# Column means of an 8192 x 8192 matrix: the first load divided by partitions

## The chip, the cores and the metric

The kernel runs on one core of a Trainium2 chip. The metric is the device time of one execution in microseconds (us). Before the change three runs took 627.25, 627.92 and 628.02 us; the median is 627.92 us. One more execution was profiled.

Engines are named as in the profile: PE is TensorE, DVE VectorE, ACT ScalarE, POOL GpSimd, SP SyncE. Sixteen DMA engines move the data between HBM and SBUF, the core's memory of 128 partitions.

## The reference

```python
def setup_inputs():
    return {"x": np.random.randn(8192, 8192).astype(np.float32)}

def reference(x):
    return np.mean(x, axis=0)
```

The input is 268.4 MB, the output 32 KB. Every element is read once and added once.

## The kernel before

The 8192 rows are 64 slabs of 128 rows. The first 62 slabs are taken as 31 pairs. For pair k, `rows(k)` (line 59) lays 256 rows out as 128 partitions with two neighbouring rows each, so a partition's share is 16,384 numbers, 64 KB that lie together in HBM. Three buffers of that size, `pairs[0]` to `pairs[2]`, take the pairs in turn.

All loads are issued by the sync queue (SP). `load(k)` (line 77) issues a pair's load: pair 0 in two parts, all partitions' first 2048 numbers (8 KB a partition) and then the remaining 14,336 (56 KB); the last three pairs (`BY_ROW`) in two halves, one row of each partition at a time; every other pair in one transfer of 128 x 64 KB. The loads of pairs 0, 1 and 2 are issued at once (line 87). From pair 3 on the queue first waits until the buffer has been read: `nc.sync.wait_ge(read, k - 2)` (line 95).

VectorE adds. `take(sem, n)` (line 56) waits until a landing semaphore has reached n and subtracts it; every DMA adds 16 when it has landed. The first addition (line 98) folds pair 0's two rows into one, in place. Then for each pair `first_rows` adds the running sum of the buffer before to the pair's first rows, and `second_rows` adds its second rows. `read` is raised behind them and lets the sync queue load the next pair. Each addition is 128 x 8192 numbers at line 54.

The last two slabs come one at a time into the buffer that is free then: the first in four transfers (line 164), the last in ten (line 167). TensorE multiplies the running sum and both slabs by a block of ones and so adds over the partitions into PSUM, piece by piece as the last slab lands; ScalarE and VectorE scale by 1/8192 and three small transfers write the result.

The edit touches only `FIRST` (line 17), `load` and the count in the first `take` (line 97):

```python
FIRST = 2048
...
        cut = FIRST if k == 0 else C if k >= n_pairs - BY_ROW else 2 * C
        for lo, hi in ((0, cut), (cut, 2 * C)):
            if lo < hi:
                sem = second[b] if lo == C else landed[b]
                ins = nc.sync.dma_start(out=pairs[b][:, lo:hi], in_=rows(k)[:, lo:hi])
...
        take(landed[0], 32)
```

## Time and profile before

| | |
|---|---|
| median of three runs | 627.92 us |
| profiled execution, its own time | 627.88 us |
| its span in the profile | 626.1 us |
| DVE busy | 533.5 us, 85% of the span, 67 instructions |
| PE busy | 14.1 us |
| bytes from HBM | 268.44 MB, 429 GB/s over the span |
| one pair addition on DVE, 128 x 8192 | 8.69 us |
| first addition starts | 22.72 us |

Windows and timelines count microseconds from the span's start. A row of a timeline gives start, length, engine, line, operation, output and input, the number of instructions, and in brackets how long the engine was idle before and what ended that. In a list of waits the numbers are the total in us, how many, and the longest. In a list of windows the columns are the stretch, its length, the busy time of PE, PEld (weight loads), DVE, ACT and POOL with the number of instructions, the granted TensorE clock, the busy share of the DMA engines and the GB/s. The bytes of a packet are counted where it starts, so a short window can show more than the engines' mean rate. In a list of DMA issues the numbers are how many, the size of one, and us from issue to landing.

### The profile page before, as it was taken

The numbers are of one execution on the slowest core, as the hardware profiler recorded it, in microseconds if no ns is written. First come the engines' busy times: TensorE is split into PE (matmuls) and PEld (weight loads), VectorE is DVE, ScalarE is ACT, GpSimd is POOL, SyncE is SP. The second block draws the span as 40 slices with busy tenths as digits, with TensorE's granted clock in tenths as the row PEclk, the third lists the DMA queues.
The fourth block names the chain that finished last, engine by engine and source line by source line (L and its number), as shares of the span: only waits on it lengthen the run. The fifth ranks groups of instructions, "written<-read, shape, count | busy, mean of one in ns | idle before, by whom it ended". The sixth has DMA issues, their size and how long they took to land. (4 is left out here: it accounts for less than half of the span.)

```text
span 626.1 us, 524 instructions
## 1 busy us (share of the span) xinstructions
PE 14.1 (2%) x108; PEld 4.8 (1%) x108; DVE 533.5 (85%) x67; ACT 4.2 (1%) x7; POOL 1.0 (0%) x6
## 2 busy tenths in 40 slices
PE   0000000000000000000000000000000000000008
PEld 0000000000000000000000000000000000000002
DVE  0538988889888899888898888988889888899995
ACT  0000000000000000000000000000000000000001
POOL 0000000000000000000000000000000000000000
PEclk9999999999999999999999999999999999999999
DMA  9999999999999999999999999999999999999997
GB/s 404 400 469 402 469 402 465 406 415 456 402 469 402 469 402 469 402 469 402 469 402 469 402 469 402 469 402 456 415 444 427 444 427 415 423 435 435 435 424 316
DMA packets 7115, 268.49 MB, mean 429 GB/s; under 512 B 957, under 2 KB 1473, under 8 KB 1866
## 3 DMA queue, kind: packets, MB, share of 16 engines
q1 hardware_dynamic: 7066, 268.45, 99.3%
q0 software_dynamic: 48, 0.02, 0.0%
q8 instruction: 1, 0.02, 0.0%
HBM read 268.44 MB, written 0.03 MB: 429 GB/s over the span
## 5 line engine op out<-in xcount | busy, mean ns | idle before, releaser
L54 DVE TENSOR_TENSOR pair<-pair,pair 128x8192 f32<-128x8192 f32 (+1 forms) x31 | 263.1, 8486 | 61.5 <-DVEq L57 60.9
L54 DVE TENSOR_TENSOR pair<-pair 128x8192 f32<-128x8192 f32 (+1 forms) x34 | 269.7, 7938 | 23.8 <-DVEq L57 22.7
L136 PE MATMUL wide<-pair,ones 128*32 128x512 f32 (+1 forms) x88 | 12.7, 673 | 609.4 <-DVE pair L54 609.1
L136 PEld LDWEIGHTS wide<-pair,ones 128*32 128x32 f32 x88 | 3.6, 127 | 616.9 <-issue 614.9
L151 ACT ACT_TABLE_LOAD x1 | 1.3, 1283 | 603.4 <-ACTq L112 603.4
L153 DVE TENSOR_SCALAR row<-narrow 1x256 f32<-1x256 f32 x2 | 0.8, 415 | 4.8 <-PE narrow L136 4.8
L136 PE MATMUL narrow<-pair,ones 128*32 128x256 f32 (+3 forms) x20 | 3.5, 387 | 0.0
L151 ACT ACTIVATE rw<-wide 128x512 f32<-128x512 f32 x3 | 1.8, 597 | 15.5 <-PE wide L136 15.5
L199 POOL DMA_DIRECT2D out_dram<-rw x1 | 0.7, 695 | 621.4 <-ACT rw L151 621.4
L136 PEld LDWEIGHTS narrow<-pair,ones 128*32 128x32 f32 x20 | 1.4, 108 | 1.6 <-issue 0.6
L151 ACT ACTIVATE row<-narrow 1x256 f32<-1x256 f32 x2 | 0.8, 377 | 0.5 <-PE narrow L136 0.5
L151 ACT ACTIVATE r<-wide 128x256 f32<-128x256 f32 x1 | 0.4, 384 | 0.3 <-PE wide L136 0.3
L92 POOL MEMSET ones<- 128x32 f32 x1 | 0.1, 124 | 0.3 <-POOLq L230 0.3
L230 POOL MEMSET const-float32-0.0<- 128x1 f32 x1 | 0.1, 98 | 0.2 <-issue 0.2
L230 POOL MEMSET const-float32-1.0<- 128x1 f32 x1 | 0.1, 98 | 0.0
L230 POOL MEMSET const-bfloat16-1.0<- 128x1 bf16 x1 | 0.1, 98 | 0.0
L230 POOL MEMSET const-uint8-127<- 128x1 uint8 x1 | 0.1, 98 | 0.0
## 6 DMA issues: line engine op xcount, KB each, us to landing
pair<-in_x_dram SPq DMA_DIRECT2D x6, 4096.0 KB, 25.6
pair<-in_x_dram SPq DMA_DIRECT2D x7, 1024.0 KB, 11.6
pair<-in_x_dram SPq DMA_DIRECT2D x1, 7168.0 KB, 21.4
pair<-in_x_dram SPq DMA_DIRECT2D x3, 512.0 KB, 16.0
pair<-in_x_dram SPq DMA_DIRECT2D x27, 29.7
pair<-in_x_dram SPq DMA_DIRECT2D x3, 128.0 KB, 11.8
pair<-in_x_dram SPq DMA_DIRECT2D x1, 80.0 KB, 7.4
pair<-in_x_dram SPq DMA_DIRECT2D x1, 48.0 KB, 5.3
```

The lines of the kernel that those rows point to most:

```text
L54: return nc.vector.tensor_tensor(out=dst, in0=a, in1=b, op=ADD)
L92: tc.declare_fence(nc.gpsimd.memset(ones, 1.0).ins, group="ahead")
L136: nc.tensor.matmul(out=dst, lhsT=ones, rhs=src, skip_group_check=True, **flags)
L151: nc.scalar.mul(out=dst, in_=src, mul=inv_r)
L153: nc.vector.tensor_scalar(out=dst, in0=src, scalar1=inv_r, scalar2=None, op0=mybir.AluOpType.mult)
L199: nc.gpsimd.dma_start(out=out[0:W3].rearrange("(n g w) -> g n w", g=GROUPS, w=512), in_=rw.rearrange("(g r) (n w) -> g r n w", r=32, w=512 ...
L230: nc = _bacc.Bacc("TRN2", target_bir_lowering=False, num_devices=1)
```

## The change

Pair 0's load is divided in another way. Before, it was cut by columns, and both parts covered all 128 partitions. After, there are three transfers: partitions 0 to 15 with their first 4096 numbers (16 KB each, 256 KB together), partitions 16 to 127 with their whole 64 KB (7 MB), and the remaining 48 KB of each of partitions 0 to 15 (768 KB). All three raise `landed[0]` by 16, so the first addition waits for 48 in place of 32. The loads of all other pairs and all that follows stay as they were; the order of instructions on PE, DVE, ACT and POOL is the same, and SP issues one transfer more.

```diff
-FIRST = 2048
+FIRST = (16, 4096)
...
     def load(k):
         b = k % 3
-        cut = FIRST if k == 0 else C if k >= n_pairs - BY_ROW else 2 * C
-        for lo, hi in ((0, cut), (cut, 2 * C)):
-            if lo < hi:
-                sem = second[b] if lo == C else landed[b]
-                ins = nc.sync.dma_start(out=pairs[b][:, lo:hi], in_=rows(k)[:, lo:hi])
-                yield ins.then_inc(sem, 16)
+        parts = [(0, P, 0, 2 * C)]
+        if k == 0:
+            p, w = FIRST
+            parts = [(0, p, 0, w), (p, P, 0, 2 * C), (0, p, w, 2 * C)]
+        elif k >= n_pairs - BY_ROW:
+            parts = [(0, P, 0, C), (0, P, C, 2 * C)]
+        for p, q, lo, hi in parts:
+            ins = nc.sync.dma_start(out=pairs[b][p:q, lo:hi], in_=rows(k)[p:q, lo:hi])
+            yield ins.then_inc(second[b] if lo == C else landed[b], 16)
...
-        take(landed[0], 32)
+        take(landed[0], 48)
```

## The prediction

> **What bounds the kernel now.** I read three things: the page's DMA rows, to see whether the transfer engines ever rest; the waits of VectorE and of the load queue, to see who waits for whom; and the first microseconds, because only the first pair's load is edited.

> The page, parts 2 and 3:

> ```profile
> DVE  0538988889888899888898888988889888899995
> DMA  9999999999999999999999999999999999999997
> q1 hardware_dynamic: 7066, 268.45, 99.3%
> HBM read 268.44 MB, written 0.03 MB: 429 GB/s over the span
> ```

> The sixteen DMA engines are busy in every slice, and the sync queue's transfers fill 99.3% of their time. In the trace's packet records, a packet of 65,536 bytes takes 2.418 us, one of 57,344 takes 2.116 us and one of 8,192 takes 0.309 us: about 27.1 GB/s for each engine, 16 x 27.1 = 434 GB/s for all. The matrix is 16.78 MB for each engine, 256 packets of 64 KB, or 256 x 2.418 = 619.0 us. The first packet starts at 1.78 us and the last load lands at 623.1 us, so the stream lasts 621.3 us with about 2 us not used.

> The waits of the sync queue, and then those of VectorE:

> ```profile
> SPq L83 <- DVEq L70: 558.2, 28, 47.9
> ...
> DVE pair L54 <- DVEq L57: 83.6, 28, 22.7
> ```

> VectorE waits 83.6 us for landed pairs (L57 is `take`, the wait on the landing semaphore). It isn't the bound: its two additions of a pair are 2 x 8.69 = 17.4 us, a pair's load 8 x 2.418 = 19.34 us. The sync queue waits for a buffer to be read, but that costs nothing so long as loads are queued ahead.

> The start, as a timeline, the same stretch by windows, and the DMA issues:

> ```profile
> 0.75 50.47 SPq L83 DMA_DIRECT2D pair<-in_x_dram  x5
> 22.72 8.69 DVE L54 TENSOR_TENSOR pair<-pair 128x8192 f32<-128x8192 f32 x1 [22.72 <-DVEq L57]
> 42.11 8.69 DVE L54 TENSOR_TENSOR pair<-pair,pair 128x8192 f32<-128x8192 f32 x1 [10.69 <-DVEq L57]
> ...
> 0.00:1.80 1.80, 0.00 (x0) 0.00 (x0) 0.00 (x0) 0.00 (x0) 0.33 (x5) 1.00 0.06 9
> 1.80:4.60 2.80, 0.00 (x0) 0.00 (x0) 0.00 (x0) 0.00 (x0) 0.00 (x0) 1.00 0.97 336
> 4.60:22.00 17.40, 0.00 (x0) 0.00 (x0) 0.00 (x0) 0.00 (x0) 0.00 (x0) 1.00 1.09 472
> ...
> pair<-in_x_dram SPq DMA_DIRECT2D x1, 7168.0 KB, 21.4
> ...
> pair<-in_x_dram SPq DMA_DIRECT2D x1, 1024.0 KB, 4.9
> ```

> The first pair comes as 1 MB (landed 4.9 us after its issue) and 7 MB. The first addition starts at 22.72 us, when both are there; the next pair is 19.4 us later, one pair at full rate. The fifth issue, the first that waits for a buffer, is at 50.9 us; the third pair's load ends about 61 us. So some 10 us of load are always queued ahead, and the engines never run dry. **Hence what the first pair's load loses or gains moves the end one for one.** From the last landing to the end, 3.0 us, only shifts.

> **The change part by part.** Before, each engine has for pair 0 eight packets of 8 KB and eight of 56 KB, all loads being 128 partitions high. After, sixteen engines share 16 partitions, then 112, then 16. That a transfer of few rows is spread one row to an engine shows at the end of this trace: the output of 4 rows (L203) gives 1 + 4 increments of its semaphore, and that of one row (L215) 1 + 1. So I take one packet of 16 KB for each engine, seven of 64 KB, then one of 48 KB.

> *Bytes and packets.* Before: 8 x 0.309 + 8 x 2.116 = 19.40 us for each engine. After, if nothing collides: 16.38 KB and 49.15 KB at 27.1 GB/s are 0.604 and 1.813 us; with the same few ns for each packet 0.61 + 7 x 2.418 + 1.82 = 19.36 us. Gain 0.04 us.

> *The start.* The first load has 16 rows in place of 128. The first packet follows its issue by 1.03 us, the engines start over 0.59 us (1.78 to 2.37), and their first packets take 0.79 us on the mean in place of 0.31. A gain is bounded by the spread and the slow packets, 0.59 + 0.48 = 1.1 us. A loss is bounded by one more issue ahead of the 112 rows, about 0.45 us (issues at 0.75, 1.22, 1.67 and 2.15). I take 0: the 16 KB packets, started at 1.8 us, end near 2.6 us, and the second load, issued at 1.22 us, has its packets at 1.22 + 1.03 = 2.25 us, so no gap; the first packets' slowness is the path filling, which stays.

> *The two loads of 16 neighbouring partitions.* In the trace no load goes to fewer than 128 partitions, so what sixteen engines lose when all write into a narrow strip has to be bounded. Lowest: nothing, if 27.1 GB/s is a limit of the engine alone. Highest: a strip of 16 partitions gets its share of the 434 GB/s, an eighth; then 1 MB takes 8 x 2.418 = 19.34 us in place of 2.42, +16.9 us. Between lie s neighbouring partitions that share one write path of an engine's speed: (s - 1) x (0.60 + 1.81) us. The 434 GB/s are 434 / 27.1 = 16 such paths, 8 partitions each; s = 8 (the highest) if a path's eight are neighbours, s = 1 if they are dealt out singly. No row tells s; as a choice between the ends I take s = 4, two runs of four to a path: 256 KB in 2.42 us in place of 0.60 (+1.81) and 768 KB in 7.25 in place of 1.81 (+5.44), together **+7.25 us**. For paths of an engine's speed speaks the packet time, 2.418 us with hardly any scatter on sixteen engines at once, where one shared pool should scatter.

> [...]

> *The load of 112 partitions.* Lowest: no collisions, 7 x 2.418 = 16.93 us, counted above. Of the sixteen paths four lose four partitions each to the strip, and twelve have all eight: a busiest path needs 8 x 2.418 = 19.34 us at least, +2.42, since an engine with seven rows in a block now strays over two or three groups of four. A path is also idle while no engine is at its rows; I take one packet more, nine: 21.76 us, **+4.84 us**. Highest: rows dealt to the engines in turn, so that at each step all write 16 neighbours: 7 x 4 packet times, 67.7 us, +50.8.

> *Order.* The rest of the strip now comes last, and the first addition waits for it (`take(landed[0], 48)`). VectorE has nothing else to do until then, and behind the addition only the next pair is queued, which comes 19.4 us later. The read counts that the sync queue waits for shift with it; if some engines come out of the first pair up to 8 us ahead of others, the 10 us of queued load still cover it. The two more issues of pair 0 and pair 1 lie beside 19 us of transfers: nothing. The instructions of the other engines are the same.

> **Sum.** 0 - 0.04 + 1.81 + 5.44 + 4.84 = +12.0 us. On the profiled execution's 627.88 us (span 626.1 and 1.8 around it; the median of the runs is 627.92, the same) this is **640.0 us**, 1.9% slower.

> **The rivals.**

> *The destination costs nothing* (the limit is the engine's own, or an engine still gets only partitions that it got before). For it: packets of 8, 56 and 64 KB all run at 27 GB/s. Against: every load measured here is spread over all partitions, so the row can't tell the two apart. 627.88 - 0.04, with the start's bounds 626.8 to 628.3; I take 627.8. This is within 0.2%, 1.26 us, about what a measurement of this kernel can tell from no change.

> *Faster.* The same, and the start gains at its upper bound: 16 rows are set out sooner than 128, the engines start together and at full rate, and 1.1 us go, which gives 626.8. It decides only from 1.26 us, so the first packet must also come 0.2 us sooner after its issue than now (1.03 us). Against it: the second load's packets can't come before 2.25 us.

> *Two to a path.* Then + 2.4 us for the strip and 0 to 2.4 for the 112: 630.3 to 632.7. *Eight to a path:* 7 x 2.42 = 16.9, and 0 to 4.8 for the 112: 644.8 to 649.6.

> *Rows dealt in turn.* With four to a path 7.25 + 50.8 = +58 us, 686 us. No row here shows which partitions an engine gets, so it keeps a chance.

> [...]

> **How the numbers follow.** Four to a path with blocks 0.66 (own range 635 for no collisions among the 112 up to 645); two to a path 0.08; eight 0.06; dealt in turn 0.07; destination free 0.10; faster 0.03. The prediction is the likeliest, 640.0. Leaving out the last three, 0.20, the range goes from 630.3 to 649.6. Slower 0.66 + 0.08 + 0.06 + 0.07 = 0.87, same 0.10, faster 0.03.

> **What the profile will show.** If I am right: the packets of 16 KB take about 2.4 us in place of 0.6, those of 48 KB about 7.2; in the 112 rows some packets take 4.8 us, twice the usual; the first addition starts some 9 to 12 us later than 22.72 and the second some 12 later than 42.11, and from there on both profiles run alike. Packets of the first pair at 27 GB/s throughout would make it wrong; so would an addition that starts late while the end does not, which would mean that the stream has slack after all.

## The result and the profile after

The changed kernel takes 648.49 us (median of six runs, 648.05 to 648.99); the kernel before took 627.86 us beside it (six runs, 627.25 to 628.02). The ratio is 1.0332, with a 95% interval of 1.0321 to 1.0343: 20.6 us slower. The direction was forecast, and the time lies in the range, but the forecast said +12.0 us.

The page of the changed kernel, the rows that answer to those of before:

```profile
DVE  0023988888988888998888998888998888899995
...
GB/s 223 247 239 442 405 450 450 405 446 446 429 421 450 442 405 450 450 401 450 446 425 425 450 442 405 450 446 405 450 446 425 425 450 442 401 434 440 423 423 297
...
q1 hardware_dynamic: 6970, 268.45, 99.2%
...
HBM read 268.44 MB, written 0.03 MB: 415 GB/s over the span
```

A slice is 647.0 / 40 = 16.2 us. The first three move 223 to 247 GB/s, about half of what the later slices move (the last one, 297, holds the end of the kernel). The queue's packets still fill 99.2% of the engines' time. That share counts a packet that crawls as busy, so it does not show the loss; the GB/s row does.

The timeline of the changed kernel from 20 to 80 us, its DMA issues of pair 0, and VectorE's wait for landed pairs:

```profile
44.84 8.69 DVE L54 TENSOR_TENSOR pair<-pair 128x8192 f32<-128x8192 f32 x1 [44.84 <-DVEq L57]
63.96 8.69 DVE L54 TENSOR_TENSOR pair<-pair,pair 128x8192 f32<-128x8192 f32 x1 [10.43 <-DVEq L57]
...
pair<-in_x_dram SPq DMA_DIRECT2D x1, 768.0 KB, 43.1
...
pair<-in_x_dram SPq DMA_DIRECT2D x1, 256.0 KB, 4.7
...
DVE pair L54 <- DVEq L57: 104.6, 28, 44.8
```

The first addition starts at 44.84 us in place of 22.72, 22.1 later; the second at 63.96 in place of 42.11, 21.9 later. VectorE's waits grow by 104.6 - 83.6 = 21.0 us and the span by 647.0 - 626.1 = 20.9. So the loss is made in pair 0 and nowhere else, and it reaches the end almost whole.

The trace's packet records show where in pair 0. I followed each of the sixteen engines from packet to packet (each starts when the one before ends) and took the n-th packets of all sixteen together; a packet of 64 KB takes 2.418 us in the later pairs (every one that starts after 150 us):

```
packet          start of the sixteen   us of one
16 KB (strip)      1.78 to  2.50       0.69 to 1.72, mean 1.27
64 KB, 1st of 7    2.51 to  3.85       5.06 to 5.96
64 KB, 2nd         7.97 to  8.90       4.77 to 4.92
64 KB, 3rd        12.73 to 13.68       fourteen 2.82 to 3.27, two 4.74 and 4.75
64 KB, 4th        16.00 to 18.41       fourteen 3.76 to 3.97, two 4.39 and 4.70
64 KB, 5th        19.75 to 22.21       4.34 to 4.82
64 KB, 6th        24.18 to 26.86       4.63 to 4.86
64 KB, 7th        28.97 to 31.49       4.36 to 5.98
48 KB (strip)     33.35 to 37.47       5.74 to 6.94, mean 6.35
pair 1, 1st       39.10 to 43.67       2.76 to 5.64, mean 4.45
pair 1, 2nd       from 44.7            2.42
```

The 48 KB packets crawl as forecast, at 6.35 us on the mean. The 112 partitions are the surprise: in five of the seven packets every engine takes 4.3 to 6.0 us, about twice 2.418. The seven take 31.2 us on the mean, where 16.93 is free and the forecast had 21.76.

### The profile page after: what moved, and what is told of

The parts are those of the page before. It is cut to its first block, busy times and chain, and to the rows that moved or that the text cites. A ratio compares the mean times of both kernels' runs of the same rounds, so it can differ in the third digit from the quotient of the medians.

```text
span 647.0 us, 525 instructions
## 1 busy us (share of the span) xinstructions
PE 14.1 (2%) x108; PEld 4.9 (1%) x108; DVE 533.5 (82%) x67; ACT 4.2 (1%) x7; POOL 1.0 (0%) x6
## 2 busy tenths in 40 slices
DMA  9999999999999999999999999999999999999997
## 3 DMA queue, kind: packets, MB, share of 16 engines
q1 hardware_dynamic: 6970, 268.45, 99.2%
HBM read 268.44 MB, written 0.03 MB: 415 GB/s over the span
## 5 line engine op out<-in xcount | busy, mean ns | idle before, releaser
L54 DVE TENSOR_TENSOR pair<-pair,pair 128x8192 f32<-128x8192 f32 (+1 forms) x31 | 263.1, 8486 | 60.3 <-DVEq L57 59.7
L54 DVE TENSOR_TENSOR pair<-pair 128x8192 f32<-128x8192 f32 (+1 forms) x34 | 269.7, 7938 | 45.9 <-DVEq L57 44.8
L140 PE MATMUL wide<-pair,ones 128*32 128x512 f32 (+1 forms) x88 | 12.6, 665 | 630.3 <-DVE pair L54 630.1
L203 POOL DMA_DIRECT2D out_dram<-rw x1 | 0.7, 695 | 642.4 <-ACT rw L155 642.4
## 6 DMA issues: line engine op xcount, KB each, us to landing
pair<-in_x_dram SPq DMA_DIRECT2D x6, 1024.0 KB, 12.7
```

Of the source, the lines that this page charges most:

```text
L54: return nc.vector.tensor_tensor(out=dst, in0=a, in1=b, op=ADD)
L140: nc.tensor.matmul(out=dst, lhsT=ones, rhs=src, skip_group_check=True, **flags)
L203: nc.gpsimd.dma_start(out=out[0:W3].rearrange("(n g w) -> g n w", g=GROUPS, w=512), in_=rw.rearrange("(g r) (n w) -> g r n w", r=32, w=512 ...
```

## The experiments

Four theories stood. A path is, as in the prediction, an assumed way into some of the partitions at one engine's speed (64 KB in 2.418 us); a meeting is two engines that write over the same path at the same time. No record shows a path: the runs show which partitions are slow together, and the two words stand for that. A is that of the prediction: an engine takes a block of neighbouring partitions, paths are shared, and only engines that meet on a path are slowed. B adds that two meetings at once slow all sixteen. C puts the cause in HBM, in which rows the engines read at the same time. D deals the rows to the engines in turn.

### The loads by themselves

This kernel only loads, and ran once: it issues nineteen loads of 64 KB rows, each waiting for the one before:

```diff
+    loads = [
+        (slice(0, 128), src[0:128]),
+        (slice(0, 16), src[128:144]),
+        (slice(32, 96), src[256:320]),
+        (slice(0, 64), src[384:448]),
+        (slice(32, 96, 4), src[512:528]),
+        (slice(28, 92, 4), src[640:656]),
+        (slice(24, 88, 4), src[768:784]),
...
+        (slice(0, 64, 4), src[1152:1168]),
+        (slice(16, 128), src[1296:1408]),
+        (slice(16, 128), eights[176:192, 0:7]),
+        (slice(0, 128), src[1536:2432:7]),
...
+        for n, (p, rows) in enumerate(loads):
+            nc.sync.dma_start(out=buf[p, :], in_=rows).then_inc(done, 16)
+            nc.sync.wait_ge(done, 16 * (n + 1))
```

> This kernel leaves the column means out: it only loads 64 KB rows into given partitions, one transfer after the other, each waiting for the one before, and writes one row back. The packet times of each transfer are the measurement; a packet alone on its path takes 2.42 us. Theory A (an engine takes a block of neighbouring partitions; four neighbours and the four 32 away share a path of 27 GB/s; only engines that meet on a path are slowed): partitions 0-15 9.7 us a packet; 32-95 2.42; 0-63 4.84; sixteen partitions in steps of four from 32, 28, 24, 20, 16 and 0 have 0, 1, 2, 3, 4 and 8 meetings, so 0, 2, 4, 6, 8 and 16 packets of 4.84 and the rest of 2.42; pairs of partitions 0 and 1, 0 and 32: 4.84; 0 and 4, 0 and 64: 2.42; partitions 0-3 9.7; partitions 16-127 about 21.8 us in all, from whichever rows of HBM. Theory B (as A, but from two meetings at a time all sixteen engines fall to the rate of those that meet): the same, but from two meetings on all sixteen packets take 4.84, and partitions 16-127 take about 30 us. Theory C (HBM is the cause: sixteen engines that read rows 7 x 64 KB apart, or next to each other, get in each other's way): the narrow loads run at 2.42 a packet wherever they read with the usual distances; partitions 16-127 are faster from groups of eight rows than from groups of seven; 128 partitions from every seventh row are slow. Theory D (rows dealt to the engines in turn): 32-95 9.7 us a packet, 0-63 9.7.

The windows of this run, each around one load's packets; the last number is GB/s. In order: 128 partitions; 0-15; 32-95; 0-63; sixteen in steps of four from 32, from 28 and from 24; from 0; 16-127; 16-127 from groups of eight rows; 128 from every seventh row:

```profile
1.90:22.40 20.50, 0.00 (x0) 1.00 0.97 409
23.70:33.30 9.60, 0.00 (x0) 1.00 0.88 109
36.00:46.70 10.70, 0.00 (x0) 1.00 0.96 392
48.20:69.10 20.90, 0.00 (x0) 1.00 0.96 201
71.10:74.60 3.50, 0.00 (x0) 1.00 0.83 300
76.10:81.30 5.20, 0.00 (x0) 1.00 0.59 202
83.40:88.60 5.20, 0.00 (x0) 1.00 0.86 202
105.30:111.00 5.70, 0.00 (x0) 1.00 0.82 184
112.50:144.50 32.00, 0.00 (x0) 1.00 0.94 229
146.60:178.20 31.60, 0.00 (x0) 1.00 0.94 232
180.00:200.50 20.50, 0.00 (x0) 1.00 0.98 409
```

The window of 128 partitions is 20.50 us long, where eight packets of 2.418 are 19.34, and a load's first packets take about 3.0 us (2.45 to 3.28 for the sixteen from 32 below), so short windows show less than the packets' own rate. Sixty-four partitions, 32-95, move at 392 GB/s, nearly as 128 do; another sixty-four, 0-63, move at 201. Only the place differs: in the words of A, 32-95 have no meeting and 0-63 have eight at a time. Sixteen neighbours move at 109, about a quarter. Their packets took 7.91 to 8.89 us, less than the 9.7 expected, and the load as a whole 9.5 us; the four partitions 0 to 3 took 7.65 to 8.71. That fits s = 4 for these partitions, and so do the pairs below.

The packet records of the loads of sixteen and of two (a record has its time and size, not its engine or partition, so which packets met is read from the number that are slow; the meetings are counted as A has them):

```
meetings  partitions            packets, us
0         in fours from 32      2.45 to 3.28
1         in fours from 28      fourteen 2.42 to 3.19, two 4.55 and 4.61
2         in fours from 24      4.04 to 4.98, all sixteen
3         in fours from 20      3.85 to 5.30
4         in fours from 16      4.37 to 5.01
8         in fours from 0       4.35 to 5.29
-         0 and 1               5.10, 4.44
-         0 and 4               3.45, 3.32
-         0 and 32              4.37, 4.94
-         0 and 64              3.32, 3.28
```

Partitions 0 and 1 are slow together (5.10 and 4.44 us), and so are 0 and 32 (4.37 and 4.94); 0 and 4 (3.45 and 3.32) and 0 and 64 (3.32 and 3.28) are not. Across the border at 64 a distance of 32 costs nothing: 32-95 ran at 392 GB/s. With one meeting two packets are slow, 4.55 and 4.61 us, and fourteen take 2.42 to 3.19. **With two, all sixteen take 4.04 to 4.98, so the twelve that by A's count meet nobody are slow too**, and with eight (4.35 to 5.29) it is hardly worse than with two. That fits theory B. Not every partition was tried singly; that the others go together in the same way is taken from the number of slow packets. The load of 16-127 takes 31.9 us from one set of rows and 31.5 from the other, where A expected 21.8 and B about 30; that speaks against A as well, and against C, which expected the two to differ. C fails also on 128 partitions from every seventh row, which ran at 409 GB/s, the rate of 128 neighbouring rows. D fails on 32-95, where it had 9.7 us a packet and the load ran at 392 GB/s.

By the same reading a load of 128 isn't dealt out in blocks of neighbours, eight to an engine: the first engine and the fifth would be 32 partitions apart at every step and meet, yet its packets after the first took 2.42 us. The records don't say which rows each engine takes there.

### Other rows of HBM in the whole kernel

```diff
+            eights = rows(0).rearrange("(g e) c -> g e c", e=8)
...
+            src = rows(k)[p:q, lo:hi]
+            if k == 0:
+                src = eights[:, 7, lo:hi] if p == 0 else eights[:, 0:7, lo:hi]
```

> As the changed kernel, but the sixteen engines read from groups of eight rows of HBM (the first seven of each group go to partitions 16-127, the eighth to 0-15), so the distance between engines is 512 KB in place of 448 KB, as in the load of 128 up to a factor of two; the partitions written are the same. Theories A and B: no difference, 648.5 within 1. Theory C: clearly another time, nearer to 628. Theory D: no difference.

It took 648.89 us in one run (before: 628.0 in one beside it). The first addition on its timeline:

```profile
44.77 8.69 DVE L54 TENSOR_TENSOR pair<-pair 128x8192 f32<-128x8192 f32 x1 [44.77 <-DVEq L57]
```

44.77 against 44.84 us: with these other rows of HBM and the same partitions nothing changes. C is out here as well.

### Two halves

```diff
-            parts = [(0, p, 0, w), (p, P, 0, 2 * C), (0, p, w, 2 * C)]
+            parts = [(0, 64, 0, 2 * C), (64, P, 0, 2 * C)]
...
-        take(landed[0], 48)
+        take(landed[0], 32)
```

> Pair 0 is loaded as partitions 0-63 and then 64-127, 64 KB each. Theories A and B: each half meets two to a path, 8 packet times of 4.84 = 38.7 us for the pair in place of 19.4, +19.3 us, 647.2. Theory C: the distances in HBM are those of the load of 128, no loss, 627.9. Theory D: four to a path, 8 x 9.67 = 77.4 us, +58 us, 686.

648.38 us in one run, +20.4 against the 628.0 beside it; forecast +19.3. The first addition and the stretch of pair 0's load:

```profile
44.31 8.69 DVE L54 TENSOR_TENSOR pair<-pair 128x8192 f32<-128x8192 f32 x1 [44.31 <-DVEq L57]
...
1.90:44.50 42.60, 0.00 (x0) 0.00 (x0) 0.19 (x1) 0.00 (x0) 0.00 (x0) 1.00 1.02 222
```

Two plain halves cost as much as the change. In the 0-63 load by itself a packet took 5.12 us and not 2 x 2.418 = 4.84 (48 of its 64 packets took 5.11 to 5.13). Over eight packets that is 2.2 us more than forecast, which the first addition shows (21.6 us late, 44.31 - 22.72); about 1.1 of it came back later, as in the changed kernel. Dealing in turn (D) would have given 686, and C no loss. A and B forecast the same here, so this run doesn't part them.

### The first small transfer undone

```diff
-            parts = [(0, p, 0, w), (p, P, 0, 2 * C), (0, p, w, 2 * C)]
+            parts = [(16, P, 0, 2 * C), (0, 16, 0, 2 * C)]
...
-        take(landed[0], 48)
+        take(landed[0], 32)
```

> Pair 0 is loaded as partitions 16-127, then partitions 0-15 with all their 64 KB in one transfer: the 256 KB ahead are undone, the narrow strip and the 112 rows stay. Theories A and B: the strip costs 9.67 in place of 2.42 us either way, so within 1.5 us of the changed kernel, 647 to 649. If the first small transfer clogs the path for the 112 rows behind it, a gain of several us, 640 or less.

649.04 us in one run, the first addition at 45.04 us:

```profile
45.04 8.69 DVE L54 TENSOR_TENSOR pair<-pair 128x8192 f32<-128x8192 f32 x1 [45.04 <-DVEq L57]
```

So the 256 KB put first are neither the cause nor a help: in one piece the strip costs about as much as in two.

### The middle first

If meetings alone decide, a division into more transfers of fewer partitions should be cheaper than the change, so long as the largest has no meeting:

```diff
-            parts = [(0, p, 0, w), (p, P, 0, 2 * C), (0, p, w, 2 * C)]
+            parts = [(32, 96, 0, 2 * C), (0, 32, 0, 2 * C), (96, P, 0, 2 * C)]
```

> Pair 0 is loaded as partitions 32-95, then 0-31, then 96-127, 64 KB each: more transfers than before, but the middle one has no two engines on a path, the outer ones two on every path. Theories A and B alike: 4 x 2.42 + 2 x 4.84 + 2 x 4.84 = 29.0 us for the pair in place of 19.4, with the 5.1 us a packet that the halves' run showed 30.2: +9.7 to +10.8, of which up to 1 us comes back later as in the changed kernel: 636.7 to 638.7. If dividing by partitions costs something of itself (a gap between transfers, rows in another order), as slow as the halves, about 648.

638.08 us (four runs, 637.99 to 638.38), ratio to before 1.0169 (1.0154 to 1.0185): 10.4 us slower, half of the change's loss. The first addition, and the windows of the middle and of the outer parts:

```profile
33.79 8.69 DVE L54 TENSOR_TENSOR pair<-pair 128x8192 f32<-128x8192 f32 x1 [33.79 <-DVEq L57]
...
2.00:12.50 10.50, 0.00 (x0) 0.00 (x0) 0.00 (x0) 0.00 (x0) 0.00 (x0) 1.00 1.02 412
12.50:33.00 20.50, 0.00 (x0) 0.00 (x0) 0.00 (x0) 0.00 (x0) 0.00 (x0) 1.00 1.08 249
```

Its packets take 2.42 us in the middle after the first (2.44 to 3.28) and 4.4 to 5.1 in the outer parts. The forecast was 636.7 to 638.7. The 10.4 us measured leave nothing for the dividing itself beyond the 9.7 to 10.8 reckoned from packets; which partitions go together decides here. A and B are alike here too.

### Not divided at all

```diff
-            parts = [(0, p, 0, w), (p, P, 0, 2 * C), (0, p, w, 2 * C)]
+            parts = [(0, P, 0, 2 * C)]
...
-        take(landed[0], 48)
+        take(landed[0], 16)
```

> Pair 0 is loaded in one transfer of 128 partitions with 64 KB, not divided at all. Nothing meets; 8 x 2.418 = 19.34 us in place of 19.40, and one issue less: 627.8, within 0.2% of the kernel before. If a small first transfer does start the stream sooner, slower by up to 1 us, 628.9.

627.76 us (eleven runs), ratio to before 1.0003 (0.9994 to 1.0012): no difference. A first load cut small starts nothing sooner here that the end would see. No division tried here beats the kernel before.

### Meetings among fewer engines

> This kernel leaves the column means out: like the first probe it only loads 64 KB rows into given partitions, one transfer after the other. In that probe packets of a load without a meeting took about 3.0 us (the first of a load is slow), those that met two to a path 4.0 to 5.3. Eight partitions in steps of eight from 32, 24, 16, 8 and 0 have 0, 1, 2, 3 and 4 meetings of two engines, with only eight engines at work. If the slowing of engines that meet nobody (theory B) comes from two paths with meetings, whatever else runs, all eight packets take 4.0 to 5.3 from two meetings on. If it comes from the total that sixteen engines ask for (half the engines leave room), the four engines that meet nobody in the load with two meetings stay at about 3.0. Four partitions of which three share a path and one is alone: the three about 6.5 to 7.5, the lone one 3.0 if a single path with a queue slows nobody else. Sixteen partitions in steps of four from 32, 28, 24, 40 repeat 0, 1, 2 and 2 meetings: none, two packets, all, all slow; sixteen in steps of seven from 11 have no meeting: 3.0 each, although every engine writes into partitions that it doesn't serve in a load of 128.

```diff
+        (slice(32, 89, 8), src[128:136]),
+        (slice(24, 81, 8), src[256:264]),
+        (slice(16, 73, 8), src[384:392]),
...
+        (slice(1, 5, 1), src[1536:1540]),
...
+        (slice(11, 117, 7), src[2432:2448]),
```

The windows: eight partitions in steps of eight from 32, 24, 16 and 0 (0, 1, 2 and 4 meetings), then sixteen in steps of seven from 11:

```profile
24.40:27.80 3.40, 0.00 (x0) 1.00 0.44 154
29.30:34.40 5.10, 0.00 (x0) 1.00 0.34 103
36.70:41.80 5.10, 0.00 (x0) 1.00 0.43 103
51.30:56.50 5.20, 0.00 (x0) 1.00 0.44 101
...
149.60:153.50 3.90, 0.00 (x0) 1.00 0.76 269
```

GB/s of a window can't tell one meeting from two, since both last as long as their slowest packet; the packets can. With one meeting two took 4.85 and 4.90 us, the other six 2.77 to 3.23. With two meetings all eight took 3.93 to 4.91; a second time one took 3.13, outside the forecast, and the other seven 3.85 to 4.68. So here the others were slowed with eight engines at work as well. Of partitions 1 to 4, three packets took 6.16 to 6.93 us and one 3.58, somewhat over the 3.0 forecast for the lone one, so three that meet hardly slowed the fourth. The loads of sixteen came out as forecast a second time: none slow from 32 (2.42 to 3.38), one pair from 28 (3.89 and 4.74, the others 2.43 to 3.30), all from 24 (3.98 to 4.99) and all from 40, where the two meetings would be 64 and 96, 68 and 100 (4.09 to 5.01). Sixteen in steps of seven, without a meeting by the same count, took 2.49 to 3.55, nearly as the sixteen from 32: there the partitions as such cost little.

## Why the prediction was right in direction and short in size

**What bounds the kernel, and that the head's loss reaches the end: right.** Pair 0's last landing came 22.1 us later (44.71 against 22.59; the signs put the first addition 9 to 12 us later), and the span grew by 20.9. What came back, 1.1 us, came back over pairs 1 to 7: in the kernel before, 64 KB packets that start between 50 and 150 us took 2.436 us on the mean and those later 2.418; after the change all took 2.418. The undivided load shows the same slow packets (2.431); the middle-first division and the other kernels with a slow first pair don't (2.418). Why was not tested.

**Bytes, packets, start, order: right, all near nothing.** The undivided load, 0.1 us from before, and strip_last, without the small first transfer and within 0.6 us of the changed kernel, bear it out. What makes a load's first packets slow (0.79 us for 8 KB in the kernel before, about 3.0 for 64 KB in the loads by themselves) no run shows; "the path filling" was the author's guess.

**The strip, +7.25 us: right,** though s = 4 was a choice between the ends there. The 16 KB and 48 KB packets took 1.27 + 6.35 us, the first packets behind them were longer by 5.31 - 4.80 = 0.51 and 4.45 - 2.42 = 2.03, together 10.16. Less the 0.53 us that the slow start had cost before too (19.93 for pair 0 on the mean engine, against 19.40 of the packets) this is 9.63, where 4 x 2.418 = 9.67 was the sum's value: +7.2 over the 2.43 without meetings. In the list of what the profile would show, the single packets were off (1.27 and 6.35 for 2.4 and 7.2), because part of the time stood in the packets behind, the 0.51 and 2.03 us.

**The 112 partitions, +4.84 us: this is the step that failed.** It measured 31.21 - 0.51 = 30.7 us, +13.8 over 16.93. The step counted packet times on the busiest path and let all other engines run on: "I take one packet more, nine." The slow packets below fit blocks of seven and four to a path, as assumed; the records show neither engine nor partition. With blocks, the first to seventh partitions of engine e (0 to 15) are 16 + 7e to 22 + 7e, and counted as in the loads by themselves these would meet:

```
packet  would meet                   the packets took
1st     16 and 51, 72 and 107        all sixteen 5.1 to 6.0 (behind the strip)
2nd     24 and 59, 80 and 115        all sixteen 4.8 to 4.9
3rd     88 and 123                   two 4.75, fourteen 2.98 on the mean
4th     68 and 103                   two 4.4 and 4.7, fourteen 3.79
5th     20 and 55, 76 and 111        all sixteen 4.3 to 4.8
6th     28 and 63, 84 and 119        all sixteen 4.6 to 4.9
7th     64 and 99, 92 and 127        4.4 to 6.0
```

Counted so, only four of sixteen engines meet at a time, but where two meetings are counted all sixteen packets took 4.3 to 6.0 us. The fourth packet fits this as well. Until 18.0 and 18.4 us the two stragglers of the third packet would still meet while two others meet in their fourth, which makes two meetings; behind that there would be one until the fifth packets begin at 19.8. Its fourteen took 3.79 us, between the 2.42 without a meeting and the 4.80 of the second packet. In the third packet, with one meeting, the fourteen took 2.98 and not 2.42; why, the runs don't tell. Nine packet times became nearly thirteen (30.7 / 2.418 = 12.7).

**Sum.** On the mean engine -0.04 + 7.2 + 13.8 = 21.0 us, less 1.1 us given back plus 1.1 by which the slowest engine lost more than the mean (22.1 against 21.0): 21.0, where the span grew by 20.9.

**The rivals.** Destination free, two to a path, eight to a path and dealt in turn all fell by the loads taken alone, "faster" by the time itself. The likeliest case, four to a path with blocks, had 635 to 645 us as its own range, and 648.49 lies outside it. The whole range held the time only through the price of "eight to a path", 644.8 to 649.6, a reason that is not the one shown. That was luck.

## What to carry to other kernels

When a load of 128 partitions already fills the DMA engines, as here (99.3% of their time, 429 GB/s), judge a division by partitions by which partitions are written at the same instant, not by bytes or by the number of transfers: 64 partitions ran at 392 GB/s at 32-95 and at 201 at 0-63. Here the load divided by columns gave 627.86 us, undivided 627.76, divided by partitions 638.08 to 649.04: by columns, or not at all. Read the GB/s row and the times of single packets: the changed kernel's queue was 99.2% busy, with 223 to 247 GB/s in its first three slices.
